# Stated orders at both ends of an attention block, and u-phase products of 512 columns over both token parts

## The chip, the cores and the metric

The kernel runs on one core of one Trainium2 chip. Time is microseconds on the device from launch to end, the median of a few executions. TensorE is called PE (its weight loads PEld), VectorE DVE, ScalarE ACT, GpSimd POOL, and SP is the sync engine, which issues most DMAs.

## The reference, cut to what matters

Two layers follow each other on 256 tokens of width 1024, all in fp32. The first is a feed-forward, a mixer, a second feed-forward and a gate (its code is not touched but for orders). The second is this:

```python
h = modulate(rmsnorm(x, norm1_g), sh1, sc1)
z = h @ w_in                          # u_pool, q, k, v, f_logit, g_a, g_b
y = sigmoid(g_a) * pool_mixer(u_pool) + sigmoid(g_b) * forgetting_attention(q, k, v, log_sigmoid(f_logit + b_f))
x = x + gt1 * (y @ w_out)
h2 = modulate(rmsnorm(x, norm2_g), sh2, sc2)
# peer_ffn: 8 heads, each picks 16 of 16384 experts by product keys
u = expert_u[ec]
a = gelu(einsum('cd,chkd->chk', xc, u), approximate=False) * wc
out = einsum('chk,chkd->cd', a, expert_v[ec])
x = x + gt2 * out
return rmsnorm(x, final_g)
```

## The kernel before

Every fp32 product is made of three: each operand is split into a high part H (rounded by ACT) and a low part L (the rest, by DVE, L289 and L290), and HL, HH and LH add up in PSUM (mm3, L314). Weights come by DMA into raw buffers (SP's queue), wload and wsplit turn them into wh and wl. The tokens are two parts, c = 0 and 1, of 128.

The experts are computed densely. In the u phase (ublock, L1684) block i of 128 multiplies 128 experts' u with all 256 tokens: fm_mm takes 8 steps of three products of 256 columns (L323 to L325), and ACT applies Gelu into row i of the tile G. DVE meanwhile finds the top 16 keys (half, cand, lookup); from about block 45 on, wgroup builds one-hot matrices (onehots, DVE, L1659 to L1662), PE turns them into 4 tokens' routing weights, and DVE multiplies these into the rows of G that are there. td is the number of tokens whose weights are there; for these a block's Gelu goes to a tile and DVE multiplies (L1693). Background work is dealt to the blocks by a credit (UC). Then the v phase multiplies G with expert v.

The order of each engine's instructions is fixed when the program is built, by a planner that simulates the engines; issue_after(x) makes the block's instructions on x's engine follow x in that engine's queue, and behind_split(c) does so after a part's last split. These are orders, not waits on other engines. Engines run their queues in order.

Around attention: ple makes the gate and the normed x; Norm.part, chunk and quads (L450 to L481) square, scale (xs), transpose four tiles into a bank, modulate them (two on ACT, two on DVE) into one tile of 512 columns, and split that into hH and hL. The attention's first product is v (wv, tm_proj with a lag of 5 weights between the parts). At its end out_step multiplies y by the output weights, ev_out adds to x, the next Norm follows, and query_w splits the query weights qw for the first four query tiles. In the query loop QORD gives the order of the first tiles; 0 to 3 are only transposed there. TAIL's last feed-forward products load their weights in ffn.

```python
def behind(f, *a):
    with tc.issue_after(ins_of(lasts["pe"])):
        return f(*a)
```

## Time and profile before

| | us |
|---|---|
| median of 3 runs | 1575.57 |
| lowest, highest | 1574.95, 1575.89 |
| the profiled execution | 1574.45 |
| its span, first to last instruction | 1572.6 |
| PE busy | 1549.9 |
| DVE busy | 1125.7 |
| ACT busy | 806.6 |
| POOL busy | 83.0 |

The span is the profiled execution without what lies around it. Busy shares are averages over stages; PE's matmuls overlap in the records, so that a matmul's price is the distance between starts. A wait stands in brackets behind an instruction, with what ended it.

### The profile page before, as it was taken

To read this page: it belongs to the slowest core of one execution; us is meant where nothing else is said; L and a number is where in the kernel's file an instruction comes from. 1 tells how busy PE (TensorE), PEld (TensorE's weight loads), DVE (VectorE), ACT (ScalarE), POOL (GpSimd) and SP (SyncE) were. 2 spreads that over 40 slices of the span, in tenths; PEclk is the share of its full clock that TensorE was granted. 3 is DMA by queue.
4 is the path that set the end of the run, shared out by engine and by line. 5 is a ranking of instruction groups with operands and counts; after the bars stand their busy time and mean duration, and the time that the engine had idled before them with its cause. 6 is when DMAs were issued, how large, how long until landed. Compare 5 with 4: busy or idle time off the path is not lost.

```text
span 1572.6 us, 27124 instructions
## 1 busy us (share of the span) xinstructions
PE 1549.9 (99%) x10317; PEld 1403.6 (89%) x10317; DVE 1125.7 (72%) x2206; ACT 806.6 (51%) x1533; POOL 83.0 (5%) x147
## 2 busy tenths in 40 slices
PE   9999999999999999999999999999999999999997
PEld 7999999879999879998899999999999877888886
DVE  7767768768866666557799988788986666555654
ACT  6444564554455656655554555544445445554543
POOL 1300011100000112011000000000000000000001
PEclk9999999999999999999999999999999999999999
DMA  8777754438976356442455655555446777666662
GB/s 315 242 259 255 246 170 135 140 104 298 337 227 228 123 189 200 134 135 94 150 162 186 187 175 165 162 158 161 161 158 199 248 227 232 191 190 195 215 189 87
DMA packets 84995, 299.94 MB, mean 191 GB/s; under 512 B 9632, under 2 KB 11264, under 8 KB 84608
## 3 DMA queue, kind: packets, MB, share of 16 engines
q1 hardware_dynamic: 80640, 290.86, 56.6%
q10 hardware_dynamic: 4224, 7.34, 1.4%
q8 instruction: 81, 1.33, 0.3%
q14 instruction: 50, 0.41, 0.1%
HBM read 294.95 MB, written 3.15 MB: 190 GB/s over the span
## 4 chain that ended last, share of the span: by engine, by line
PE 89%; DMA 4%; DVE 3%; ACT 2%; issue 1%; POOL 0%; ACTq 0%; POOLq 0%; DVEq 0%
PE mm L323 15%; PE mm L324 15%; PE mm L325 15%; PE acc L319 12%; PE acc L321 11%; PE acc L320 11%; DMA raw<-in_pv 2%; DMA raw<-in_wmod 2%; DVE wl L290 1%; PE acc L1673 1%; ACT wh L289 1%; PE acc L1674 1%; PE acc L925 1%; PE sc L1290 1%; PE mm L1565 0%
## 5 line engine op out<-in xcount | busy, mean ns | idle before, releaser
L289 ACT ACTIVATE wh<-raw 128x1024 fp32r<-128x1024 f32 (+3 forms) x605 | 528.3, 896 | 539.1 <-PE mm L324 251.9
L290 DVE TENSOR_TENSOR wl<-raw,wh 128x1024 fp32r<-128x1024 f32 (+3 forms) x605 | 611.2, 1027 | 264.7 <-ACT wh L289 260.0
L323 PE MATMUL mm<-hL,wh 128*128 128x256 f32 x1976 | 565.4, 286 | 0.0
L325 PE MATMUL mm<-hH,wl 128*128 128x256 f32 x1976 | 560.2, 284 | 0.0
L324 PE MATMUL mm<-hH,wh 128*128 128x256 f32 x1976 | 560.0, 283 | 0.0
L323 PEld LDWEIGHTS mm<-hL,wh 128*128 128x128 f32 x1976 | 377.6, 191 | 2.7
L324 PEld LDWEIGHTS mm<-hH,wh 128*128 128x128 f32 x1976 | 377.9, 191 | 2.0
L325 PEld LDWEIGHTS mm<-hH,wl 128*128 128x128 f32 x1976 | 377.4, 191 | 0.5
L319 PE MATMUL acc<-wh,aL 128*128 128x512 f32 x648 | 255.9, 395 | 1.6 <-DVE aL L290 1.6
L320 PE MATMUL acc<-wh,aH 128*128 128x512 f32 x648 | 253.0, 390 | 0.0
L321 PE MATMUL acc<-wl,aH 128*128 128x512 f32 x648 | 252.9, 392 | 0.0
L321 PEld LDWEIGHTS acc<-wl,aH 128*128 128x128 f32 x648 | 121.7, 188 | 28.2 <-issue 0.2
L319 PEld LDWEIGHTS acc<-wh,aL 128*128 128x128 f32 x648 | 121.9, 188 | 27.4 <-DVE aL L290 2.8
L320 PEld LDWEIGHTS acc<-wh,aH 128*128 128x128 f32 x648 | 121.8, 188 | 26.2 <-issue 0.5
L319 PE MATMUL acc<-wh,hL 128*128 128x512 f32 x224 | 89.3, 401 | 3.1 <-ACT wh L289 1.7
L320 PE MATMUL acc<-wh,hH 128*128 128x512 f32 x224 | 87.4, 392 | 0.0
L321 PE MATMUL acc<-wl,hH 128*128 128x512 f32 (+1 forms) x224 | 85.8, 391 | 0.0
L624 DVE SCALAR_TENSOR_TENSOR macc<-raw,col,macc 128x1024 f32<-128x1024 f32 x28 | 36.1, 1288 | 29.4 <-DMA raw<-in_wmod 29.3
L290 DVE TENSOR_TENSOR aL<-G,aH 128x256 fp32r<-128x256 f32 x128 | 53.6, 419 | 3.4 <-ACT aH L289 3.4
L319 PEld LDWEIGHTS acc<-wh,hL 128*128 128x128 f32 x224 | 42.5, 190 | 13.0 <-ACT wh L289 3.2
L289 ACT ACTIVATE aH<-G 128x256 fp32r<-128x256 f32 x128 | 51.2, 401 | 4.0 <-PE acc L321 4.0
L587 ACT ACTIVATE sg<-sg 128x256 f32<-128x256 f32 x36 | 14.8, 411 | 71.0 <-DVE sg L586 68.1
(469 smaller groups left out, 1620.9 us busy)
## 6 DMA issues: line engine op xcount, KB each, us to landing
raw<-in_pu SPq DMA_DIRECT2D x128, 512.0 KB, 3.5
raw<-in_pv SPq DMA_DIRECT2D x128, 512.0 KB, 4.3
raw<-in_wmod SPq DMA_DIRECT2D x48, 512.0 KB, 4.8
raw<-in_w1gu SPq DMA_DIRECT2D x36, 512.0 KB, 4.4
raw<-in_w2gu SPq DMA_DIRECT2D x36, 512.0 KB, 4.9
raw<-in_w1d SPq DMA_DIRECT2D x22, 512.0 KB, 4.8
raw<-in_w2d SPq DMA_DIRECT2D x22, 512.0 KB, 4.5
raw<-in_wout SPq DMA_DIRECT2D x16, 512.0 KB, 3.6
```

The costliest lines, as they stand in the source:

```text
L289: lasts["high"] = act.activation(H, src, AF.Copy)
L290: lasts["low"] = dve.tensor_sub(L, src, H.bitcast(F32))
L319: mm_(ps, aL, bH, start=start, stop=False)
L320: mm_(ps, aH, bH, start=False, stop=False)
L321: lasts["pe"] = mm_(ps, aH, bL, start=False, stop=stop)
L323: mm_(ps, aH, bL, start=start, stop=False)
L324: mm_(ps, aH, bH, start=False, stop=False)
L325: mm_(ps, aL, bH, start=False, stop=stop)
L624: dve.scalar_tensor_tensor(macc[j], raw, K("c", k), macc[j], op0=OP.mult, op1=OP.add)
L925: mm_(ps[:, j, c], k[pr][:, j, sl], q[pr][:, j, sl], start=True, stop=True)
L1290: mm_(ps[:, o:o + n], qa[:, hd, c * 128:c * 128 + 128], ka[:, hd, 0:n], start=True, stop=False)
L1673: mm_(ps[:, j], H[:, j], O[:, j], start=True, stop=False)
```

## The change

The u product. ublock uses fm_wide: a weight's high half is multiplied with hH and hL side by side (512 columns, hH in the bank's first half, hL in the second), its low half with hH alone (256). The halves of the bank must then be added. While no routing weights are there (td is 0), ACT copies both halves into two rows of G, POOL adds them, ACT applies Gelu in place. Later ACT copies the second half, DVE adds the first from PSUM, ACT applies Gelu, and POOL, not DVE, multiplies by the routing weights. A block's evacuation comes behind the background work dealt to it. hH and hL become one tile for this, in every norm.

Orders. wv's splits, the scaling of xr, wpool's DMA, the last query weights' splits and ev_out(1, 1) get stated places; a quad's modulated tile becomes two; three of four query weights get their L from POOL; head 15 uses a bank of "sc"; QORD interleaves. The first feed-forward's lag goes from 4 to 2, its and the second's tail weights follow the last split, and x, col and w1t are loaded in another order. Left out of the diff: where hH, hL and yH, yL become halves of one tile.

```diff
@@ -35,8 +35,9 @@
-FLAG = (4, 4)
+FLAG = (2, 4)
 TLW = (3, 3)
+TLA = (2, 2)
@@ -55,7 +56,7 @@
-QORD = [4, 5, 0, 1, 2, 3]
+QORD = [4, 0, 5, 1, 6, 2, 7, 3]
@@ -264,12 +265,12 @@
     xv = A["x"].rearrange("(c p) d -> p c d", p=128)
-    def xload(c, j):
-        nc.sync.dma_start(xr[:, c, j * 512:j * 512 + 512], xv[:, c, j * 512:j * 512 + 512])
...
-    xload(0, 0)
+    def xload(c, a, b):
+        nc.sync.dma_start(xr[:, c, a:b], xv[:, c, a:b])
+    xload(0, 0, 128)
     nc.sync.dma_start(cst[:, 0:128], A["cst"][:, 0:128])
-    nc.scalar.dma_start(col, A["col"])
+    xload(0, 128, 512)
@@ -329,6 +330,19 @@
+    def fm_wide(ps, w, hw, nk=8):
+        for k in range(nk):
+            wH, wL = (w[i][:, k * 128:(k + 1) * 128] for i in range(2))
+            low = lambda: mm_(ps[:, 0], wL, hw[:, 0, k], start=False, stop=False)
+            if k == nk - 1:
+                low()
+            mm_(ps, wH, hw[:, :, k], start=k == 0, stop=k == nk - 1)
+            if k < nk - 1:
+                low()
@@ -437,12 +451,12 @@
         def __init__(self, hp, gain, shift=None):
-            self.hH = hp.tile([128, 8, 256], F32R, tag="hH", name="hH")
-            self.hL = hp.tile([128, 8, 256], F32R, tag="hL", name="hL")
+            self.both = hp.tile([128, 2, 8, 256], F32R, tag="h", name="h")
+            self.hH, self.hL = self.both[:, 0], self.both[:, 1]
             self.gain, self.shift = gain, shift
...
             self.s, self.xs, self.last_xs, self.mp = {}, {}, {}, nxp
-            self.last_hH, self.last_hL = {}, {}
+            self.last_hH, self.last_hL, self.late = {}, {}, {}
@@ -460,25 +474,32 @@
         def quads(self, c):
...
                 self.quad(c, q)
+            for k in list(self.late) if c else ():
+                with self.behind_split(1), tc.high_priority(offset=-300):
+                    self.late.pop(k)()
             return self.last_pe
...
-            sl, qs = slice(c * 128, (c + 1) * 128), slice(4 * q, 4 * q + 4)
+            sl = slice(c * 128, (c + 1) * 128)
             x = self.xs[c]
...
                 self.last_pe = nc.tensor.transpose(bk[:, i], x[:, dt * 128:(dt + 1) * 128], ident)
-            m = self.mp.tile([128, 4, 128], F32, tag="mod", name="mod", bufs=2)
-            for i in range(4):
-                dt = 4 * q + i
-                if i < 2:
-                    act.activation(m[:, i], bk[:, i], AF.Identity, scale=self.gain(dt), bias=self.shift(dt))
-                else:
-                    dve.tensor_scalar(m[:, i], bk[:, i], self.gain(dt), self.shift(dt), op0=OP.mult, op1=OP.add)
-            self.last_hH[c] = act.activation(self.hH[:, qs, sl], m, AF.Copy)
-            self.last_hL[c] = dve.tensor_sub(self.hL[:, qs, sl], m, self.hH[:, qs, sl].bitcast(F32))
+            for u in range(2):
+                m = self.mp.tile([128, 2, 128], F32, tag="mod%d" % u, name="mod", bufs=2)
+                for i in range(2):
+                    dt = 4 * q + 2 * u + i
+                    if u == 0:
+                        act.activation(m[:, i], bk[:, 2 * u + i], AF.Identity, scale=self.gain(dt),
+                                       bias=self.shift(dt))
+                    else:
+                        dve.tensor_scalar(m[:, i], bk[:, 2 * u + i], self.gain(dt), self.shift(dt),
+                                          op0=OP.mult, op1=OP.add)
+                us = slice(4 * q + 2 * u, 4 * q + 2 * u + 2)
+                self.last_hH[c] = act.activation(self.hH[:, us, sl], m, AF.Copy)
+                self.last_hL[c] = dve.tensor_sub(self.hL[:, us, sl], m, self.hH[:, us, sl].bitcast(F32))
@@ -590,6 +611,7 @@
                 aH = p.tile([128, 256], F32R, tag="aH", name="aH", bufs=TAIL[i - 1] + 2)
...
                 split(a, aH, aL)
+                last_a = lasts["high"], lasts["low"]
                 pend.append((f, (aH, aL)))
@@ -598,7 +620,13 @@
             cut["n"] = CUT4[i - 1]
-            W = [wload(wd[f_], 1024, pw if n_ >= len(pend) - TLW[i - 1] else None) for n_, (f_, _) in enumerate(pend)]
+            W = []
+            for n_, (f_, _) in enumerate(pend):
+                with ExitStack() as order_:
+                    if n_ >= TLA[i - 1]:
+                        for a_ in last_a:
+                            order_.enter_context(tc.issue_after(ins_of(a_)))
+                    W.append(wload(wd[f_], 1024, pw if n_ >= len(pend) - TLW[i - 1] else None))
@@ -698,12 +726,13 @@
             q.dma_start(raw1[k][:, i:i + m], A["w1t"][k][:, i:i + m])
     wraw1(0, 2, nc.scalar)
-    wraw1(1, 2, nc.scalar)
-    xload(1, 0)
+    nc.scalar.dma_start(col, A["col"])
+    wraw1(1, 2)
+    xload(1, 0, 512)
     wraw1(2)
-    xload(0, 1)
     wraw1(3)
-    xload(1, 1)
+    xload(0, 512, 1024)
+    xload(1, 512, 1024)
     nc.sync.dma_start(cst[:, 128:], A["cst"][:, 128:])
@@ -1155,6 +1184,8 @@
     def ple(nin, nout):
...
             st, hg = {}, {}
+            squares, sums = nout.squares, nout.sums = {}, {}
+            nout.gates = {}
@@ -1164,7 +1195,7 @@
                 t = p.tile([128, 512], F32, tag="pg", name="pg")
...
                 with nout.behind_split(0) if c else nullcontext():
-                    act.activation(t, ps, AF.Tanh, scale=nin.half[c])
+                    nout.gates[c] = act.activation(t, ps, AF.Tanh, scale=nin.half[c])
                     dve.scalar_tensor_tensor(t, t, 1.0, proj[:, c, sl], op0=OP.add, op1=OP.mult)
@@ -1182,7 +1213,7 @@
                     pool.tensor_scalar(ss[:, 5:6], ss[:, 0:1], EPS, D * EPS * EPS, op0=OP.mult, op1=OP.add)
...
                 else:
-                    act.activation(sq[:, 0:256], g[:, 0:256], AF.Square, accum_out=ss[:, 3:4])
+                    squares[c] = act.activation(sq[:, 0:256], g[:, 0:256], AF.Square, accum_out=ss[:, 3:4])
                     dve.scalar_tensor_tensor(sq[:, 256:], g[:, 256:], 1.0, g[:, 256:], op0=OP.mult, op1=OP.mult,
@@ -1191,14 +1222,19 @@
                 ss = st[c]
-                v = nrm.tile([128, 2], F32, tag="q1", name="q1")
-                dve.tensor_scalar(v[:, 0:1], ss[:, 3:4], ss[:, 4:5], ss[:, 5:6], op0=OP.add, op1=OP.add)
+                v = nrm.tile([128, 1], F32, tag="q1", name="q1")
+                sums[c] = dve.tensor_scalar(v[:, 0:1], ss[:, 3:4], ss[:, 4:5], ss[:, 5:6], op0=OP.add, op1=OP.add)
                 pool.tensor_tensor(v[:, 0:1], v[:, 0:1], mhalf[:, 0:1], op=OP.pow)
                 nout.chunk(c, hg[c], v[:, 0:1])
-                pool.tensor_scalar(v[:, 1:2], ss[:, 0:1], ss[:, 1:2], D * EPS, op0=OP.add, op1=OP.add)
-                pool.tensor_tensor(v[:, 1:2], v[:, 1:2], mhalf[:, 0:1], op=OP.pow)
-                with tc.high_priority(offset=-300), tc.issue_after(ins_of(nout.last_xs[c])):
-                    dve.tensor_scalar(xr[:, c], hg[c], v[:, 1:2], 32.0, op0=OP.mult, op1=OP.mult)
+                u = nrm.tile([128, 1], F32, tag="q2", name="q2")
+                def late():
+                    pool.tensor_scalar(u, ss[:, 0:1], ss[:, 1:2], D * EPS, op0=OP.add, op1=OP.add)
+                    pool.tensor_tensor(u, u, mhalf[:, 0:1], op=OP.pow)
+                    pool.tensor_scalar(u, u, 32.0, None, op0=OP.mult)
+                    act.activation(xr[:, c], hg[c], AF.Copy, scale=u)
+                nout.late[c] = late
@@ -1251,7 +1287,14 @@
         def wv(kt):
-            with tc.issue_after(ins_of(nin.last_xs[0])) if kt < 5 else nin.behind_split(0):
+            with ExitStack() as order_:
+                if kt > 0:
+                    order_.enter_context(tc.issue_after(ins_of(nin.squares[0])))
+                    order_.enter_context(tc.issue_after(ins_of(nin.sums[0] if kt < 2 else nin.last_xs[0])))
+                if kt > 1:
+                    order_.enter_context(nin.behind_split(0))
+                if kt > 2:
+                    order_.enter_context(tc.issue_after(ins_of(nin.gates[1])))
                 return wload(A["wv"][kt])
@@ -1312,7 +1355,7 @@
         def head4(hd, pT, sums):
-            po = bank("mm" if hd >= POM else "pt", (128, 2, 64))
+            po = bank("sc" if hd == 15 else "mm" if hd >= POM else "pt", (128, 2, 64))
@@ -1323,7 +1366,8 @@
             wp = sm.tile([128, 256], F32, tag="wp", name="wp")
-            nc.scalar.dma_start(wp, A["wpool"][:, g * 256:(g + 1) * 256])
+            with nin.behind_split(1) if g < 2 else nullcontext():
+                nc.scalar.dma_start(wp, A["wpool"][:, g * 256:(g + 1) * 256])
@@ -1459,7 +1503,11 @@
                 sl = slice(j * 512, (j + 1) * 512)
-                split(raw[:, sl], H[:, sl], L[:, sl])
+                if i == 0:
+                    split(raw[:, sl], H[:, sl], L[:, sl])
+                else:
+                    act.activation(H[:, sl], raw[:, sl], AF.Copy)
+                    pool.tensor_sub(L[:, sl], raw[:, sl], H[:, sl].bitcast(F32))
             qw.append((H, L))
@@ -1470,12 +1518,13 @@
         query_w(0)
-        with tc.issue_after(ins_of(pT_read)), tc.issue_after(ins_of(ysum)):
+        with tc.issue_after(ins_of(pT_read)):
             query_w(1)
-        with tc.issue_after(ins_of(yhigh)), tc.issue_after(ins_of(ysum)):
+        with tc.issue_after(ins_of(yhigh)):
             query_w(2)
             query_w(3)
-        ev_out(1, 1, acc[1, 1])
+        with tc.issue_after(ins_of(nout.last_hL[0])):
+            ev_out(1, 1, acc[1, 1])
@@ -1682,15 +1731,29 @@
             state["td"] = t0 + 4
         def ublock(i):
-            ps = mm_bank((128, 256))
-            fm_mm(ps, wload(A["pu"][i]), h)
+            ps = mm_bank((128, 2, 256))
+            fm_wide(ps, wload(A["pu"][i]), n6.both)
+            return ps
+        def upart(i, ps):
             td = state["td"]
+            if td == 0:
+                j = 86 + i % 2
+                rows = G[:, i:j + 1:j - i]
+                act.activation(rows, ps, AF.Copy)
+                pool.tensor_add(G[:, i], G[:, i], G[:, j])
+                act.activation(G[:, i], G[:, i], AF.Gelu)
+                assert i < 86
+                state["cur"] = i + 1
+                return
+            u = ps_.tile([128, 256], F32, tag="ge", name="ge")
+            act.activation(u, ps[:, 1], AF.Copy)
+            dve.tensor_add(u, ps[:, 0], u)
             if td < 256:
-                act.activation(G[:, i, td:], ps[:, td:], AF.Gelu)
-            if td > 0:
-                t = ps_.tile([128, 256], F32, tag="ge", name="ge")
-                act.activation(t[:, 0:td], ps[:, 0:td], AF.Gelu)
-                dve.tensor_mul(G[:, i, 0:td], t[:, 0:td], G[:, i, 0:td])
+                act.activation(G[:, i, td:], u[:, td:], AF.Gelu)
+            act.activation(u[:, 0:td], u[:, 0:td], AF.Gelu)
+            pool.tensor_mul(G[:, i, 0:td], u[:, 0:td], G[:, i, 0:td])
             state["cur"] = i + 1
@@ -1711,7 +1774,7 @@
             if i < 16:
...
             else:
-                ublock(0)
+                upart(0, ublock(0))
@@ -1735,8 +1798,9 @@
         for i in range(1, 128):
-            ublock(i)
+            ps = ublock(i)
             run(UC)
+            upart(i, ps)
         while bg:
...
```

## Rows read from the trace of the kernel before

**Rows 1.** The page: busy time and share of each engine; the chain by engine.

```profile
PE 1549.9 (99%) x10317; PEld 1403.6 (89%) x10317; DVE 1125.7 (72%) x2206; ACT 806.6 (51%) x1533; POOL 83.0 (5%) x147
...
PE 89%; DMA 4%; DVE 3%; ACT 2%; issue 1%; POOL 0%; ACTq 0%; POOLq 0%; DVEq 0%
```

**Rows 2.** Busy time by stretch of the u phase: us, engines, PEclk, DMA.

```profile
806.00:898.70 92.70, 92.70 (x775) 92.70 (x774) 88.16 (x368) 47.21 (x70) 0.00 (x0) 1.00 0.58 182
898.70:943.40 44.70, 44.70 (x383) 44.66 (x382) 37.84 (x61) 23.72 (x38) 0.00 (x0) 1.00 0.56 177
946.10:1184.80 238.70, 238.70 (x2230) 236.06 (x2229) 205.02 (x340) 114.62 (x283) 0.00 (x0) 1.00 0.51 160
```

**Rows 3.** Timeline of PE in a u block: start us, us, what.

```profile
899.80 0.28 PE L323 MATMUL mm<-hL,wh 128*128 128x256 f32 x1
...
906.88 0.28 PE L325 MATMUL mm<-hH,wl 128*128 128x256 f32 x1
```

**Rows 4.** Timeline of PE in the v phase.

```profile
1399.77 0.39 PE L320 MATMUL acc<-wh,aH 128*128 128x512 f32 x1
...
1403.89 0.39 PE L320 MATMUL acc<-wh,aH 128*128 128x512 f32 x1
```

**Rows 5.** Start of attention: timelines of PE and DVE, one stretch's busy times.

```profile
553.93 1.95 PE L643 MATMUL fill<-cst,macc 128*128 128x1 f32 x16 [1.84 <-DVE modc L644]
...
568.49 0.50 PE L319 MATMUL acc<-wh,hL 128*128 128x512 f32 x1 [1.28 <-DVE hL L481]
...
547.03 4.90 DVE L290 TENSOR_TENSOR wl<-raw,wh 128x512 fp32r<-128x512 f32 x8
...
553.79 1.36 DVE L479 TENSOR_SCALAR mod<-mm,modc 128x128 f32<-128x128 f32 x4
...
555.50:559.60 4.10, 3.96 (x13) 3.16 (x13) 4.10 (x9) 3.18 (x7) 0.00 (x0) 0.58 0.34 125
```

**Rows 6.** Waits of PE, 725 to 772 us: for what, us, times, longest.

```profile
PE acc L319 <- DVE hL L481: 3.1, 2, 1.7
PE mm L1317 <- DVE gb L1321: 0.7, 1, 0.7
PE mm L1565 <- ACT qT L1557: 0.6, 1, 0.6
PE mm L472 <- DVE xs L458: 0.6, 1, 0.6
PE acc L319 <- DVE yL L1385: 0.6, 1, 0.6
```

**Rows 7.** Waits of PE, 0 to 20 us.

```profile
PE acc L319 <- ACT wh L289: 1.4, 3, 0.7
```

**Rows 8.** Timeline of PE at the mixer's input products, 512 and 384 columns.

```profile
210.03 0.39 PE L319 MATMUL acc<-wh,hL 128*128 128x512 f32 x1
...
210.73 0.33 PE L319 MATMUL acc<-wh,hL 128*128 128x384 f32 x1
...
211.26 1.62 PE L643 MATMUL fill<-cst,macc 128*128 128x1 f32 x14
```

**Rows 9.** Groups of instructions, whole run: count, busy us, mean ns, idle before.

```profile
L586 DVE TENSOR_TENSOR sg<-mm,R 128x256 f32<-128x256 f32 x36 | 15.1, 420 | 5.1 <-PE mm L325 5.1
```

**Rows 10.** Groups of DVE's instructions, 946.1 to 1184.8 us.

```profile
L290 DVE TENSOR_TENSOR wl<-raw,wh 128x1024 fp32r<-128x1024 f32 x72 | 88.1, 1224 | 33.5 <-ACT wh L289 33.5
...
L1693 DVE TENSOR_TENSOR G<-ge,G 128x8 f32<-128x8 f32 (+35 forms) x72 | 20.2, 280 | 0.0
```

**Rows 11.** Timelines of DVE and POOL where a POOL product meets splits; POOL alone.

```profile
607.71 0.69 DVE L290 TENSOR_TENSOR wl<-raw,wh 128x512 fp32r<-128x512 f32 x1
...
608.73 1.83 DVE L290 TENSOR_TENSOR wl<-raw,wh 128x512 fp32r<-128x512 f32 x2
...
608.89 1.11 POOL L1351 TENSOR_TENSOR ga<-ga,y 128x256 f32<-128x256 f32 x1 [1.65 <-DVE y L1350]
...
603.03 0.61 POOL L1337 TENSOR_TENSOR psum__6605<-pu 128x255 f32<-128x255 f32 x1
```

More of the change, by code (lines that the diff above doesn't have):

```diff
@@ L494, in __init__ @@
         def __init__(self, hp, gain):
-            self.hH = hp.tile([128, 8, 256], F32R, tag="hH", name="hH")
-            self.hL = hp.tile([128, 8, 256], F32R, tag="hL", name="hL")
+            self.both = hp.tile([128, 2, 8, 256], F32R, tag="h", name="h")
+            self.hH, self.hL = self.both[:, 0], self.both[:, 1]
             self.gain, self.h = gain, (self.hH, self.hL)
@@ L799, in mixer @@
         vm = m.tile([128, 2, 512], F32, name="vm")
-        yH = hA.tile([128, 8, 256], F32R, tag="hH", name="yH")
-        yL = hA.tile([128, 8, 256], F32R, tag="hL", name="yL")
+        y_ = hA.tile([128, 2, 8, 256], F32R, tag="h", name="yH")
+        yH, yL = y_[:, 0], y_[:, 1]
         latent = {}
@@ L1373, in attention @@
         set_psum(acc=2, mm=2, sc=2, pt=2)
-        yH = hA.tile([128, 8, 256], F32R, tag="hH", name="yH2")
-        yL = hA.tile([128, 8, 256], F32R, tag="hL", name="yL2")
+        y_ = hA.tile([128, 2, 8, 256], F32R, tag="h", name="yH2")
+        yH, yL = y_[:, 0], y_[:, 1]
         def y_tile(dt):
@@ L1764, in peer @@
             if i == 96:
-                hs = [hB.tile([128, 2, 1024], F32R, tag=t, name="w" + t) for t in ("hH", "hL")]
+                hs_ = hB.tile([128, 2, 2, 1024], F32R, tag="h", name="wh_")
+                hs = [hs_[:, 0], hs_[:, 1]]
                 for k in range(2):
```

## Prediction, made before the changed kernel was run

> **What bounds the kernel now.** I read the page's busy shares and chain first. TensorE (PE) is busy 99% of the span and carries 89% of the chain that ended last [rows 1], so a saving counts only where it shortens PE's work or closes a hole in it. Next came stretches by time. The u phase, 128 blocks between 806 and 1208 us, has no PE hole, VectorE (DVE) at 95% in its first 32 blocks and at 86% later, ScalarE (ACT) near half, GpSimd (POOL) at zero [rows 2]. Here a block's price is its matmul count times their spacing, and DVE is the next engine behind. Last came the spacing of matmul starts (a busy PE is no PE at its peak) and PE's waits at the seams. 60 matmuls of 256 columns start in the 7.08 us between two rows, 59 steps of 0.120 us [rows 3]; 18 steps of 512 columns take 4.12 us, 0.229 each [rows 4]. What PE loses by waiting lies at the two ends of the attention block [rows 5, 6] and, less, at the start [rows 7].
>
> **The u product.** A block has 8 steps of 3 products of 256 columns, 3 x 0.120 = 0.360 us a step. fm_wide has one product of 512 (weight high half against both token parts) and one of 256, 0.229 + 0.120 = 0.349 us. So 0.011 us a step, 0.088 a block, **11.3 us** over 128 blocks if PE stays the bound. No run of alternating 512 and 256 columns stands in the trace. The nearest alternates 512 and 384: three of 512 take 0.70 us and three of 384 take 0.53 [rows 8], so each keeps its own spacing and the weight loads stay hidden. That the moving operand is now two pieces a distance apart is not shown; I take it as free, with 0 us of gain as the bound (at 0.240 a wide product, nothing is saved).
>
> The Trainium skill's page "TensorE: Matmul & The Clock Gate" (Back-to-back issue gap) gives a spacing of N/2.4 + 2.5 ns, a much smaller fixed part than the 13 to 16 ns left here after 106.7 and 213.3. By it a step would save 2.5 ns and the phase 2.6 us. The rows decide for the larger figure.
>
> **What it moves to other engines.** Blocks before routing (45 of them): ACT copies 512 columns out of PSUM, POOL adds the two rows of G, ACT applies Gelu. Blocks after (83): ACT copies 256, DVE adds from PSUM, ACT applies Gelu, POOL multiplies instead of DVE. No row prices ACT's 512-column copy; DVE's PSUM pass of 256 columns at 0.42 us [rows 9] puts it between 0.4 and 0.9. ACT is idle (92.70 - 47.21) / 32 = 1.4 us a block [rows 2], so it has room. The copy shares ACT's queue with the next weight split (wh) and the Gelu now waits there for POOL or DVE; queued behind that Gelu are later splits. Three weight buffers are some two blocks of lead, 5.6 us, so I cost this at nothing; if the lead is eaten, each block pays the overrun.
>
> DVE: in the 73 blocks of 946 to 1185 us it is busy 205.0 us [rows 2]. It loses the multiply, 20.2, and gains 73 x 0.42 = 30.7 [rows 9, 10]: 215.5 us, against PE's 238.7 - 73 x 0.088 = 232.3. Slack 16.8 us, 0.23 a block. In the first 32 blocks DVE's own work is unchanged at 88.2 against PE's 92.7 - 2.8 = 89.9: slack 1.7 us, 0.05 a block.
>
> **POOL against DVE** uses up that slack. Alone, a POOL add of 255 columns takes 0.61 us. At 608.89 one met DVE splits of 512 columns: it took 1.11, and the two splits took 1.83 together where one takes 0.69 [rows 11]. So POOL first waited for the running split, and then DVE's next one waited some 0.55 us. Bounds per block: 0 (a following operation that isn't held) to 0.55 (each time), for columns in proportion; the multiply's width grows from 4 to 256, so its mean bound is 0.3. I take 0.07 before routing. POOL's add comes after ACT's copy; about half of DVE's time there is the split (1.22 of 2.75 us a block), and behind it follow searches on one stream. A hit in the other half holds the next split only if that begins within 0.6 us: 0.6 x 0.6 / 2 / 2.79 = 0.065, an estimate that rests on the searches not being held, which no row shows. After routing I take 0.18, half the time a full hold. Then 32 x 0.07 = 2.2 just exceeds the slack of 1.7, and 73 x 0.18 = 13 stays below 16.8. Unevenness between blocks costs some more: I keep **9.5** of 11.3 us.
>
> The Trainium skill's "SBUF — State Buffer" (Who interferes with whom) speaks against this part: a DVE instruction with two SBUF inputs and a GpSimd one that reads SBUF hold a shared port exclusively, the later fully blocked. The rows at 608 agree. Taken at its worst, on every block, it is the slower rival below.
>
> **Start of attention.** PE waits 1.84 us at 553.93, because the modulation of the first token part (DVE, 553.79) sits behind eight split halves of wv that run from 547.03 [rows 5]. After that hole, and sixteen one-column products behind it, the granted clock is 0.58 on the mean of 555.5 to 559.6, so mostly the lower of its two levels, 1.2 and 2.4 GHz [rows 5]: (1 - 0.58) x 4.1 = 1.7 us. A further 1.28 us are lost at 568.49 for the second part's hL. The change puts wv's splits from kt 2 on behind the first part's split, moves the scaling of xr from DVE to ACT and out of the way, and halves the modulation tiles. The moved splits are then late next: PE needs a wv every 1.37 us (six products of 0.229), DVE makes one in 1.2 [rows 10], beside the second part's norm. The splits hold their raw buffers longer, so SP's loads of later wv wait for them; wp's DMA goes behind the second split and is needed far later. Of 4.8 us I take **3.5**; bounds +1 (starved of wv) and -4.8.
>
> **End of attention.** PE waits 3.1 us for hL, 0.7 for head 15's bank, 0.6 for yL, 0.6 for xs [rows 6]. Halving the quads lets the first half of hH and hL start after two modulations, not four (0.7 us of the 1.36 [rows 5]) and with passes of half the width (0.3 us each on ACT and DVE, an estimate from 0.69 for 512 columns [rows 11]): about 1.2 us for each of the two parts. Head 15 gets its own bank, and DVE loses six splits of qw. These go to POOL, at twice 0.61 about 1.2 us each, 7 us, in front of the norm's small POOL steps; xr's adds have two SBUF inputs and may be held. Of 5.0 us I take **3.0**; bounds +1.5 and -4.5.
>
> **Small ones.** At the start PE waits 1.4 us for wh [rows 7]. A first x piece of a quarter, w1t before col on ACT's queue, w1t 1 on SP's and a lag of 2 may close it, while col, now behind, feeds the first scaling: I take 0.5 (bounds +1, -1.4). Interleaving the short queries with long ones touches the 0.6 us wait for qT [rows 6]: 0.5 (bounds 0, -0.8). The tail loads of the feed-forward only get an order behind the last split; PE's work queued there hides them: nothing, or up to 1 us if a split comes late.
>
> **Sum** against the profiled execution, 1574.45 us (span 1572.6 and 1.85 around it): -9.5 - 3.5 - 3.0 - 0.5 - 0.5 = -17.0, 1557.5. The median stands 1.1 above it: **1559 us**.
>
> **The rivals.**
> Slower: DVE becomes the u phase's bound because POOL holds it in every block. For: the phase's first 32 blocks have 0.05 us of slack, and the rows at 608. Against: the searches have one stream, and the multiply is short at first. Price: 32 blocks at 88.2 + 17.6 = 105.8 against 92.7, +13.1; the next 13, 37.8 + 7.2 = 45 against 44.7, +0.3; the 73, 215.5 + 22 = 237.5 against 238.7, -1.2; the last ten, some +1 for bunching. It decides once the hold passes 0.05 us a block before routing. With the seams' -7.5 it gives +6, and with the seams at half, +10: 1582 to 1586, 1583 as its time. Chance 0.14.
> The u phase gives nothing (DVE and PE in balance, or the wide product at 0.240): -7.5, 1568. For: slack after routing is 0.23 us a block on average, less where lookups fall. Chance 0.15, a third of it with weak seams, near no change.
> The seams give nothing, a new wait (wv late, POOL's queue) taking the place of each old one: -9.5, 1566. For: both seams fill DVE almost wholly. Chance 0.15.
> Spacing with a 2.5 ns fixed part at either width: the u phase saves 2.6, in all -10.1, 1565. Against it stand both spacings. Chance 0.05. (The rule of the TensorE page.)
> The forecast has 0.48, with its own range of 1553 to 1565; 0.03 is left for no change by mishaps.
>
> **How the numbers follow.** With every bound met the sum is -11.3 - 4.8 - 4.5 - 1.4 - 0.8 = -22.8, 1551.6 and at the median 1552.8; 1552 is the low end. The high end leaves out most of the slower rival and takes in a u phase with half its hold and seams at nothing: 1579. A measurement of this kernel tells 0.2%, about 3 us, from no change. Faster: 0.48 + 0.15 + 0.05 + 0.10 = 0.78, less a little, 0.77. Same: 0.05 + 0.03 + 0.01 = 0.09. Slower: 0.14.
>
> **What would show it.** Spacing in the u phase of 0.229 and 0.120 in turn, and blocks of 2.79 us before routing; PE holes there with releaser DVE wl would mean the lock. DVE splits longer than 1.22 us beside POOL rows count its price. At 552 us PE should go on without a hole and at a full clock; a wait for wl there would be the new one. At 749 and 757 the waits for hL should halve. The prediction is wrong if blocks take 2.88 us or more.

## The result, and the profile after

The changed kernel takes 1584.1 us in the median of 6 runs (1580.73 to 1586.59), the kernel before 1575.26 us on the same chip: **slower by 0.56%, ratio 1.0056 [1.0044, 1.0068]**. Forecast were 1559 us and a gain. Its profiled execution took 1582.17 us (span 1580.3), 7.7 us more than the one of before.

The page of the changed kernel, busy time and share by engine, answers to [rows 1]:

```profile
PE 1550.5 (98%) x9293; PEld 1348.1 (85%) x9293; DVE 1152.3 (73%) x2207; ACT 869.0 (55%) x1673; POOL 217.4 (14%) x283
...
PE 90%; DMA 3%; DVE 3%; ACT 2%; issue 1%; POOL 0%; ACTq 0%; POOLq 0%; DVEq 0%
```

PE has 1024 products fewer and is busy as long as before: a product's busy time overlaps the next one's, so it tells nothing of the gain. PE still bounds. Two stretches of the u phase (busy us by engine, PEclk, DMA; [rows 2]) and a timeline of PE inside it ([rows 3, 4]):

```profile
820.00:898.00 78.00, 78.00 (x446) 67.94 (x445) 74.86 (x322) 55.44 (x88) 20.56 (x27) 1.00 0.55 180
952.00:1190.00 238.00, 238.00 (x1685) 204.99 (x1684) 229.47 (x352) 148.37 (x361) 68.71 (x73) 1.00 0.50 163
```
```profile
879.69 0.40 PE L343 MATMUL mm<-h,wh 128*128 128x512 f32 x1
...
885.33 0.40 PE L343 MATMUL mm<-h,wh 128*128 128x512 f32 x1
```

PE has no hole there and the clock is full, though DVE is at 96%. The two starts are 16 steps apart: 5.64 / 16 = 0.3525 us a step, where 0.360 stood before and 0.349 was costed.

PE's waits in the other stretches: 0 to 20 us ([rows 7]), 180 to 200 us (before: none), 550 to 580 us ([rows 5]), 735 to 800 us ([rows 6]); what waited, for what, us in total, times, longest:

```profile
PE mm L527 <- DMA xr<-in_x: 1.7, 1, 1.7
PE acc L320 <- ACT wh L290: 1.6, 1, 1.6
```
```profile
PE acc L320 <- ACT wh L290: 2.4, 1, 2.4
```
```profile
PE mm L489 <- DVE xs L472: 3.6, 1, 3.6
```
```profile
PE mm L1614 <- ACT qT L1606: 3.0, 4, 1.1
PE acc L320 <- DVE yH L1429: 2.4, 1, 2.4
PE acc L320 <- DVE h L502: 1.8, 2, 0.9
```

The old holes are gone or halved (552 us, head 15's bank, hL at 749 and 757), and each seam has a new one. To add them up with the slower clock behind them, take **PE's loss** in a stretch: the sum of the distances between neighbouring starts, less 0.229 us behind a product of 512 fp32 columns, 0.120 behind one of 256, and the median of its form behind any other. A loss near 0 means that PE ran at its best spacing. Worked out from the PE rows of each trace, in us (before_again is a second profile of the kernel before; the other names are the experiments'):

```
                        0-20  180-200  540-580  700-800  800-1220
before                   2.9    -0.1      5.6      8.5       3.3
before_again             2.6    -0.1      5.6      8.5       3.3
the changed kernel       5.6     4.4      6.3     13.2       8.4
u_alone                  4.3     5.1      6.7      8.6       8.7
u_again                  3.4     7.4      6.7      8.5       8.7
orders_alone             3.9     0.3      6.2     13.3       3.3
four_off                 2.9     2.9      5.3      8.2       8.7
four_off_again           2.6     6.9      6.3      8.2       8.6
start_off                2.9     3.1      5.3     13.2       8.4
qord_off                 5.7     1.9      5.3     10.2       8.4
qw_on_dve                5.0     0.6      4.9     11.3       8.4
tail_order_off           4.4     6.3      4.4     11.7       8.4
```

With 11.3 us costed off the u phase, the changed kernel's losses there and at the seams stand 5.1 + 2.7 + 4.5 + 0.7 + 4.7 = 17.7 us above those of before: +6.4 of the 7.7 us.

### The profile page after: what moved, and what is told of

The parts are those of the page before. It is cut to its first block, busy times and chain, and to the rows that moved or that the text cites. A ratio compares the mean times of both kernels' runs of the same rounds, so it can differ in the third digit from the quotient of the medians.

```text
span 1580.3 us, 25425 instructions
## 1 busy us (share of the span) xinstructions
PE 1550.5 (98%) x9293; PEld 1348.1 (85%) x9293; DVE 1152.3 (73%) x2207; ACT 869.0 (55%) x1673; POOL 217.4 (14%) x283
## 4 chain that ended last, share of the span: by engine, by line
PE 90%; DMA 3%; DVE 3%; ACT 2%; issue 1%; POOL 0%; ACTq 0%; POOLq 0%; DVEq 0%
PE mm L343 15%; PE acc L320 13%; PE acc L322 12%; PE acc L321 12%; PE mm L340 8%; PE mm L324 7%; PE mm L325 7%; PE mm L326 7%; DMA raw<-in_wmod 2%; DVE wl L291 2%; PE acc L1722 1%; ACT wh L290 1%; PE acc L1723 1%; PE acc L954 1%; PE sc L1333 1%
## 5 line engine op out<-in xcount | busy, mean ns | idle before, releaser
L343 PE MATMUL mm<-h,wh 128*128 128x512 f32 x1024 | 359.9, 399 | 0.0
L324 PE MATMUL mm<-h,wh 128*128 128x256 f32 (+1 forms) x952 | 271.4, 285 | 0.0
L326 PE MATMUL mm<-h,wl 128*128 128x256 f32 (+1 forms) x952 | 270.1, 284 | 0.0
L340 PE MATMUL mm<-h,wl 128*128 128x256 f32 x1024 | 268.9, 283 | 1.0 <-DVE wl L291 1.0
L325 PE MATMUL mm<-h,wh 128*128 128x256 f32 (+1 forms) x952 | 269.4, 283 | 0.0
L343 PEld LDWEIGHTS mm<-h,wh 128*128 128x128 f32 x1024 | 186.1, 188 | 33.2
L340 PEld LDWEIGHTS mm<-h,wl 128*128 128x128 f32 x1024 | 193.2, 189 | 12.8 <-DVE wl L291 3.1
L324 PEld LDWEIGHTS mm<-h,wh 128*128 128x128 f32 (+1 forms) x952 | 181.3, 190 | 2.8
L325 PEld LDWEIGHTS mm<-h,wh 128*128 128x128 f32 (+1 forms) x952 | 181.3, 190 | 2.3
L326 PEld LDWEIGHTS mm<-h,wl 128*128 128x128 f32 (+1 forms) x952 | 181.2, 190 | 0.4
L320 PE MATMUL acc<-wh,h 128*128 128x512 f32 (+1 forms) x224 | 89.7, 404 | 1.9 <-ACT wh L290 1.9
L321 PE MATMUL acc<-wh,h 128*128 128x512 f32 (+1 forms) x224 | 88.4, 397 | 0.0
L322 PE MATMUL acc<-wl,h 128*128 128x512 f32 (+1 forms) x224 | 85.6, 394 | 0.0
```

The lines of the kernel that those rows point to most:

```text
L320: mm_(ps, aL, bH, start=start, stop=False)
L321: mm_(ps, aH, bH, start=False, stop=False)
L322: lasts["pe"] = mm_(ps, aH, bL, start=False, stop=stop)
L324: mm_(ps, aH, bL, start=start, stop=False)
L325: mm_(ps, aH, bH, start=False, stop=False)
L326: mm_(ps, aL, bH, start=False, stop=stop)
```

## The experiments

Ratios are to the kernel before, timed on the same chip, with 95% intervals. 0.001 is 1.6 us.

### The u products alone, the orders alone

u_alone is the kernel before with the three new pieces of the u phase:

```diff
-            ps = mm_bank((128, 256))
-            fm_mm(ps, wload(A["pu"][i]), h)
+            ps = mm_bank((128, 2, 256))
+            fm_wide(ps, wload(A["pu"][i]), n6.both)
+            return ps
...
-            ublock(i)
+            ps = ublock(i)
             run(UC)
+            upart(i, ps)
```

> The kernel before with the new u products alone (fm_wide, upart, hH and hL as halves of one tile); every order as before. Theory (the u phase gained, the orders lost): in the two traces the stretch from the last qw product to the v phase took 445.0 us before and 441.8 after, with 2.9 us of new waits for qT inside it, so the u phase gave about 6.1 us and this kernel takes 1575.3 - 6 = 1569 us (1565 to 1571). Rival (POOL holding DVE eats the gain, the orders cost little): 1575 us or more, with PE waits for wl in the blocks.

orders_alone is the changed kernel with these lines and ublock's evacuation as before.

> The changed kernel with the u products as before; all of the new orders stay. Theory: the orders cost 13.8 us up to the end of the query stage, so 1575.3 + 13.8 = 1589 us (1586 to 1592), 5 to 6 us slower than the changed kernel. Rival (the u phase is what lost): 1575 to 1580, faster than the changed kernel.

Measured: u_alone **1573.33 us, 0.9993 [0.9982, 1.0003]**; orders_alone **1583.07 us, 1.0053 [1.0038, 1.0068]**. That the orders are what loses is the theory's reading, but its size was not: 8.3 us, where 13.8 were said and 1586 us was its least. The u products bring 1 us, between the two readings, with an interval that takes in no change. In their own stage they do gain; timelines of PE, last qw product and first product of the v phase, of before and of u_alone:

```profile
762.81 0.39 PE L321 MATMUL acc<-qw,hH 128*128 128x512 f32 x1
...
1207.81 0.39 PE L319 MATMUL acc<-wh,aL 128*128 128x512 f32 x1
```
```profile
770.56 0.40 PE L321 MATMUL acc<-qw,h 128*128 128x512 f32 x1
...
1209.67 0.40 PE L319 MATMUL acc<-wh,aL 128*128 128x512 f32 x1
```

445.0 us before, 439.1 here: 5.9 us less. But the last qw product starts 7.8 us later, and of that 5.2 us are lost at 180 to 200 us (and 1.4 at 0 to 20, 1.1 at 540 to 580). That is in the first feed-forward, where the two programs are the same instruction for instruction, waits included.

### Loads that land late in the first feed-forward

> The kernel before with the u products alone, profiled a second time. Its instructions up to 235 us stand in the order of the kernel before on PE, ACT, DVE and SP, and yet its first profile had a hole of 2.4 us at 192 us (loads landing late in the feed-forward's tail) that the kernel before does not show. Theory (a load stream near its limit, whose lateness differs from one execution to the next): the hole's length differs by over 1 us between the two profiles of this same kernel. Rival (something of the u products makes the loads late every time): a hole of 2.4 us again, pT issued at 181.7 us again. In both the stretch from the last qw product to the v phase is 439 us, as in the first.

> The kernel before, profiled a second time. Its first profile shows no PE hole between 180 and 200 us and pT issued at 176.6 us; the two profiles of the kernel with the u products alone show 5.1 and 7.4 us lost there and pT at 181.7 and 182.6, with the same instructions in the same order up to then. Theory (the lateness of this load stream differs from one execution to the next): here a loss of 1 us or more at 180 to 200 us, or pT over 1 us off 176.6. Rival (it belongs to the kernels with the new u products): under 0.3 us lost, pT at 176 to 177.

u_again lost 7.4 us there, before_again nothing, with pT issued at 182.6 and 174.2 us. Each run bears out something of both readings. The lateness does differ between executions: u_alone and u_again, one program, lost 5.1 and 7.4 us, and the issue of pT in the kernel before moved by 2.4 us. But whether PE loses anything there goes with the program. Here the issues of DMAs (KB each, median us to landing) between 40 and 170 us, of before and of u_again:

```profile
raw<-in_w1gu SPq DMA_DIRECT2D x28, 512.0 KB, 4.3
raw<-in_w1d SPq DMA_DIRECT2D x18, 512.0 KB, 4.7
```
```profile
raw<-in_w1gu SPq DMA_DIRECT2D x29, 512.0 KB, 4.6
raw<-in_w1d SPq DMA_DIRECT2D x16, 512.0 KB, 5.1
```

As I read it, weights that take 0.3 us longer delay the buffers they sit in, and so SP's next loads; by the tail the stream is 5 us behind, and ACT's and DVE's splits of late weights stand ahead of the last gate. Is it the new products that do this?

```diff
-            fm_mm(ps, wload(A["pu"][i]), h)
+            w = wload(A["pu"][i])
+            for k in range(8):
+                mm_(ps, w[0][:, k * 128:(k + 1) * 128], h[0][:, k], start=k == 0, stop=False)
+                mm_(ps, w[1][:, k * 128:(k + 1) * 128], h[0][:, k], start=False, stop=k == 7)
```

> The kernel before with the third product of each u step (weight high half by hL) left out, so that its output is off by that part; no other change, and every engine's instructions up to the u phase at 800 us are the same as before. Theory (the loads of the first feed-forward land late in any program that is built otherwise later on): 2 us or more lost at 180 to 200 us, weight loads of the feed-forward (40 to 170 us) landing in 4.6 us or more on the mean, against 4.50 and 4.46 in the two profiles of the kernel before and 4.74 and 4.89 with the new u products alone. Rival (it belongs to the new u products themselves, or was chance): nothing lost there, 4.4 to 4.5 us.

Its SP and PE timelines (pT's load; PE's start with its wait), beside SP's of before:

```profile
180.03 0.33 SPq L294 DMA_DIRECT2D raw<-in_pT  x1
...
193.44 0.80 PE L319 MATMUL acc<-wh,aL 128*128 128x512 f32 x1 [3.17 <-DVE aL L290]
```
```profile
176.57 0.33 SPq L294 DMA_DIRECT2D raw<-in_pT  x1
```

6.6 us lost, loads at 4.72 us on the mean (4.50 and 4.46 in the two profiles of the kernel before), in one profile. So it isn't the new products: a program that is the same for its first 800 us and other behind them has its loads landing later in the first 200. The length of PE's program was the first candidate.

```diff
                 done(c, j * 512, j * 512 + 512, acc[c][j], g2)
+        ps = mm_bank((128, 8))
+        with tc.issue_after(ins_of(lasts["pe"])):
+            for q in range(1024):
+                mm_(ps[:, q % 8:q % 8 + 1], C("ones", 0, 128), C("ones", 0, 1), start=True, stop=True)
```

> The kernel before with the new u products alone, and 1024 products of one column put behind the last product of the program, so that PE's program is as long again as in the kernel before; all that stands ahead of them is the same (the time grows by the length of these products and is not compared). Theory (the length of PE's program decides whether the first feed-forward's loads land late): under 0.3 us lost at 180 to 200 us, loads landing in 4.5 us on the mean. Rival (another difference between the programs, or chance): 2 us or more lost there, 4.6 us or more.

4.3 us lost, 4.64 us: the length doesn't decide. Nor are there more loads of instructions: between 40 and 170 us each of these traces has 7 or 8 packets on the larger of the two queues for them. The profiles were taken on several chips, but the timings of u_alone and of the kernel before, on one chip, differ by only 1 us where the u stage gained 5.9. **Why the loads land late in these programs stays open.** Nor is late landing the whole story: the changed kernel's loads, which start in another order, land in 4.52 us on the mean, those of tail_order_off in 4.56, and yet 4.4 and 6.3 us are lost there.

What it costs was tried by moving four loads away, M0 from 20 to 16, on the best version (below) and on the kernel before.

> The version with four orders undone, with M0 at 16: four of the 20 wmod loads that run through the first feed-forward (2 MB, about 8 us of its load stream) move to the second. Theory (that stream is near its limit, and its tail lands late): the hole at 190 us, 2.9 us with the clock behind it, goes, 1572.5 - 3 = 1569.5 us or less. Rival (the loads are late whatever is queued ahead of them, or the second feed-forward now has the hole): 1572.5 us or more.

> The kernel before with M0 at 16 and nothing else. Theory (the kernel before has no such hole to lose): within 1 us of the kernel before, 1575 us. Rival (fewer loads help by themselves): 1572 us or less, which would then also explain a gain of the run with four orders undone.

The first: 0.9994 [0.9984, 1.0004]. The hole at 190 us is gone (loss 0.2), but 2 us are lost anew at 47 us and 2 at 560, so no gain: the rival's time, by new holes. The second: 1.0019 [1.0010, 1.0027], slower by 3 us, outside both expectations. It loses 7.2 us at 540 to 580, 1.6 more than the kernel before, and 1.3 more at 20 to 100: the moved loads cost more where they go.

### Four orders undone, together and one by one

four_off undoes TLA, the start (FLAG and the loads), QORD and POOL's L of the query weights:

```diff
-FLAG = (2, 4)
+FLAG = (4, 4)
-TLA = (2, 2)
+TLA = (9, 9)
-QORD = [4, 0, 5, 1, 6, 2, 7, 3]
+QORD = [4, 5, 0, 1, 2, 3]
-    xload(0, 0, 128)
+    xload(0, 0, 512)
     nc.sync.dma_start(cst[:, 0:128], A["cst"][:, 0:128])
-    xload(0, 128, 512)
+    nc.scalar.dma_start(col, A["col"])
...
-    nc.scalar.dma_start(col, A["col"])
-    wraw1(1, 2)
+    wraw1(1, 2, nc.scalar)
...
-                if i == 0:
-                    split(raw[:, sl], H[:, sl], L[:, sl])
-                else:
-                    act.activation(H[:, sl], raw[:, sl], AF.Copy)
-                    pool.tensor_sub(L[:, sl], raw[:, sl], H[:, sl].bitcast(F32))
+                split(raw[:, sl], H[:, sl], L[:, sl])
```

> The changed kernel with four orders undone: the tail weights (TLA), the start (FLAG, x, col and w1t), QORD, and L of the query weights from POOL. The u products and the orders at both ends of attention stay. Theory: 4.4 + 2.7 + 2.9 + 2.0 = 12.0 us come back, 1584.1 - 12.0 = 1572 us (1569 to 1575). Rival (these seams only trade places with what follows, or the spread of the changed kernel is its u phase's): 1580 to 1584.

**1572.55 us, 0.9981 [0.9971, 0.9991]**: 11.8 us below the changed kernel, where the theory had 12.0. In part that is luck: by PE's loss 2.7 us came back at the start and 5.0 at 700 to 800 us, as it said, but only 1.5 of the 4.4 at 180 to 200, and 1.0 at 540 to 580 that it did not have. Each alone, from the changed kernel:

> The changed kernel with TLA at (9, 9): the tail weights of the feed-forwards follow no stated order, as before. Theory (the splits held behind the last split keep the raw buffers, so pT and wpp land late and block ACT and DVE ahead of the last gate): the 2.4 us hole at 192 us and the lower clock behind it go, 4.4 us in all, 1584.1 - 4.4 = 1579.7 us, and SP issues pT some 4 us earlier. Rival (the hole comes from the lag of 2 in FLAG or from the loads being late in any order): the hole stays, 1584.

> The changed kernel with the start as before: FLAG at (4, 4), x in pieces of 512, col ahead of w1t, w1t 1 on ACT's queue. Theory (each seam's loss in the trace is lost in the end too): PE's wait for the second x piece at 4.7 us and a part of the wait for wh go, 2.7 us, 1584.1 - 2.7 = 1581.4 us. Rival (one of the four undone orders carries most of the 11.5 us that they are worth together): either 1584, or under 1578 where the start is that one.

> The changed kernel with QORD as before. Theory: the four waits for qT between 776 and 793 us (3.6 us of PE waits in all, against one of 0.6 before) go, 1584.1 - 2.9 = 1581.2 us. Rival: 1584 where the waits only move to a later step, or under 1578 where this is the order that carries most of the 11.5 us.

> The changed kernel with L of all query weights made by DVE as before, none by POOL. Theory (POOL's subtractions hold DVE's yL split and its add to xr for 1.1 us each, 1.77 and 1.79 where 0.69 is usual): both take 0.69 again, the 2.4 us wait for yH at 747 us shrinks to 1.3 or less, and the clock behind it falls less: 1584.1 - 2.0 = 1582 us. Rival (the six splits more on DVE stand ahead of the norm, as before): 1584 or more. Third reading: under 1578 where this order carries most of the 11.5 us.

```
                 ratio    interval             us against 1.0056   in its own stretch
tail_order_off   1.0049   [1.0033, 1.0065]     -1.1                +1.9
start_off        1.0002   [0.9989, 1.0016]     -8.5                -2.7
qord_off         1.0028   [1.0016, 1.0039]     -4.4                -3.0
qw_on_dve        1.0036   [1.0024, 1.0047]     -3.2                -1.9
```

The tail order is not what makes the hole at 192 us: without it 6.3 us are lost there, and my first reading of the trace was wrong. (Profiles of one program differ there by 2 to 4 us, so the +1.9 is no price.) The four add up to 17.2 us where the four together gave 11.8, so at least one of them is not worth what it shows alone. QORD and the query weights cost about what their stretch shows; the waits of 765 to 800 us in qord_off, and of 735 to 770 in qw_on_dve:

```profile
PE mm L1614 <- ACT qT L1606: 0.6, 1, 0.6
```
```profile
PE acc L320 <- DVE yH L1429: 1.3, 1, 1.3
```

One wait for qT instead of four of 3.0, and yH 1.3 instead of 2.4. Where POOL's subtractions hold DVE is seen in the changed kernel's timelines of DVE and POOL ([rows 11]):

```profile
744.17 3.57 DVE L291 TENSOR_TENSOR wl<-raw,wh 128x512 fp32r<-128x512 f32 x4
747.66 0.41 DVE L1429 TENSOR_TENSOR yH<-mm,yH 128x256 fp32r<-128x256 f32 x1
...
750.17 1.79 DVE L1435 TENSOR_TENSOR xr<-gt,xr 128x512 f32<-128x512 f32 x1
```
```profile
745.82 5.59 POOL L1510 TENSOR_TENSOR qw<-raw,qw 128x512 fp32r<-128x512 f32 x4 [4.11 <-ACT qw L1509]
```

Four splits take 3.57 us, where four take 2.49 at 567.05 (a row shown below), and the add to xr takes 1.79 where 0.69 is usual: one of the four splits, and the add, are each held by 1.1 us while POOL's row runs. yH, which has one input in PSUM, takes its usual 0.41 beside it. The Trainium skill's "SBUF — State Buffer" (Who interferes with whom) says that a DVE instruction with two SBUF inputs contends with a GpSimd one that reads SBUF, by an exclusive lock; the trace agrees, with 1.1 us for each of these two.

The start is the odd one: 8.5 us in time, 2.7 in its stretch. Two kernels took it apart. lag_off undoes FLAG alone, x_in_one_piece the split of the first x piece alone:

```diff
-    xload(0, 0, 128)
+    xload(0, 0, 512)
...
-    xload(0, 128, 512)
```

> The changed kernel with FLAG alone at (4, 4), the lag of the first feed-forward as before; x, col and w1t still in the new order. With both undone the kernel took 0.54 percent less than the changed one, about 8 us. Theory (a lag of 2 leaves the first down product less lead over its loads, and the lead is then short for the whole of the feed-forward): 1584.1 - 6 = 1578 us or less. Rival (the load order: the second x piece lands late, and PE starts its first products late and at the lower clock): over 1581 us, and the wait at 4.7 us stays in either case.

> The changed kernel with its first load of x in one piece of 512 columns again instead of 128 and 384; col, w1t and the other pieces stay in the new order. Theory (the second piece, behind cst on SP's queue, lands at 6.6 us and starts PE's lateness): the wait at 4.7 us goes, 1584.1 - 3 = 1581 us or less. Rival (w1t 1 on SP's queue behind x, and the first w1t alone on ACT's, make wh late): the wait moves to wh at 7 to 9 us, 1584 us.

lag_off: 1.0054 [1.0041, 1.0067], so the lag is nothing. x_in_one_piece: 1.0024 [1.0014, 1.0033], 5 us less, the time that the theory had; but its wait moves as the rival said, from x to wh, and its loss at 0 to 20 us stays (5.8). Waits of 0 to 20 us in x_in_one_piece and in start_off:

```profile
PE acc L319 <- ACT wh L289: 4.0, 1, 4.0
```
```profile
PE acc L320 <- ACT wh L290: 1.0, 3, 0.7
```

The profiled execution of x_in_one_piece, 1584.84 us, is the slowest of its 11, so its trace does not show where the 5 us come from. Of the start's 8.5 us the lag is then nothing and the small x piece some 5; about 3 are left for the places of the other first loads (col, w1t, the later x pieces), which no run varied alone. Only 2.7 us are seen at PE in the first 20 us, and the profiled executions of start_off and of the changed kernel are only 4.5 us apart: the way of the rest is not shown.

### The start of attention, and the wide product

wv_order_off is four_off with wv's splits in the order of before.

```diff
-            with ExitStack() as order_:
...
-                return wload(A["wv"][kt])
+            with tc.issue_after(ins_of(nin.last_xs[0])) if kt < 5 else nin.behind_split(0):
+                return wload(A["wv"][kt])
```

> The version with four orders undone, with wv's splits too in the order of the kernel before (the first five behind the first part's xs, the rest behind its split). Theory (the order only trades the hole at 552 us for one of the same size at 568, where the second part's norm stands among the wv splits): a hole of 1.8 us at 554 us again, the wait for xs at 568 gone or below 1.3, and the same time, 1572.5 us within 1.5. Rival (the forecast's term): 3.5 us slower than the version with four orders undone, 1576 us.

0.9992 [0.9982, 1.0002], 1573.86 us: the theory's time, with a hole of 1.2 us where it had 1.8. PE's waits of 540 to 580 us in it, and in four_off:

```profile
PE fill L671 <- DVE modc L672: 1.2, 1, 1.2
PE acc L320 <- DVE h L502: 0.9, 1, 0.9
PE mm L489 <- DVE xs L472: 0.6, 1, 0.6
```
```profile
PE mm L489 <- DVE xs L472: 3.7, 1, 3.7
```

Losses 4.9 and 5.3 us: three small holes against one large. Where the large one comes from, in the changed kernel's DVE timeline, and the clock behind it, 0.51 and so almost all at the lower of its two levels, 1.2 and 2.4 GHz:

```profile
567.05 2.49 DVE L291 TENSOR_TENSOR wl<-raw,wh 128x512 fp32r<-128x512 f32 x4
569.46 0.41 DVE L1217 SCALAR_TENSOR_TENSOR sq<-hg 128x256 bf16<-128x256 f32 x1
...
572.23 0.88 DVE L472 TENSOR_SCALAR xs<-hg,q 128x512 f32<-128x512 f32 x2 [1.62 <-POOL q L1227]
```
```profile
572.70:578.00 5.30, 5.23 (x17) 4.42 (x18) 3.21 (x10) 4.03 (x10) 0.00 (x0) 0.51 0.05 19
```

The second part's square stands behind wv's splits, POOL's power behind that, xs at its end; PE is through with the wv products queued ahead of it by 568.7 us.

wide_in_one_piece is four_off with hH and hL of a step side by side:

```diff
-            self.both = hp.tile([128, 2, 8, 256], F32R, tag="h", name="h")
-            self.hH, self.hL = self.both[:, 0], self.both[:, 1]
+            self.both = hp.tile([128, 8, 2, 256], F32R, tag="h", name="h")
+            self.hH, self.hL = self.both[:, :, 0], self.both[:, :, 1]
```

> The version with four orders undone, with hH and hL of a step side by side, so that a wide product's 512 columns are one piece instead of two that lie 2048 columns apart; the instructions and their order are the same. In the two traces with the new u products a wide product and the low one behind it take 0.2352 + 0.1176 = 0.3528 us where 0.229 + 0.120 = 0.349 was costed. Theory (the two pieces cost it): 0.349 a step, 1024 x 0.0038 = 3.9 us less, 0.9981 - 0.0025 = 0.9956 of the kernel before, 1568.6 us. Rival (the change of width between two products costs it): 0.3528 again, 1572.5 us.

Its 16 steps between two rows take 886.19 - 880.55 = 5.64 us, 0.3525 a step again:

```profile
880.55 0.40 PE L343 MATMUL mm<-h,wh 128*128 128x512 f32 x1
...
886.19 0.40 PE L343 MATMUL mm<-h,wh 128*128 128x512 f32 x1
```

The two pieces cost nothing; the rival, the change of width, is left, but was not varied by itself. The time, 0.9999 [0.9987, 1.0010], is 2 us above four_off's with the same instructions in the same order. So four_off was timed again:

> The version with four orders undone, measured a second time. Theory (it is faster than the kernel before by 0.1 to 0.3 percent, the u products' 6 us less what the loads and the ends of attention take back): 0.998 again, 1572 us beside 1575. Rival (measurements of this kernel scatter by 0.2 percent from one chip or session to the next): 0.9995 or more.

0.9991 [0.9982, 1.0000], between the two readings. Both measurements put it below the kernel before, by 3 and 1.4 us; it is the best of the versions, by hardly more than can be told.

## Why the prediction was wrong, step by step

**The u product's spacing** was mis-sized. Costed: 0.229 + 0.120 = 0.349 us a step, from products of one width [rows 3, 4]. Measured: 0.3525, so 7.7 us over 1024 steps, not 11.3. [rows 8] had it: three of 512 in 0.70 are 0.233 each, not 0.229, in a row of alternating widths; I read it as "keeps its own spacing". The forecast's sign of being wrong, blocks of 2.88 us, did not come: a block takes 8 x 0.3525 = 2.82. The Trainium skill's "TensorE: Matmul & The Clock Gate" (Back-to-back issue gap) gives N/2.4 + 2.5 ns for products taken singly, which would make the pair 0.325 us, an estimate; the trace does not agree, with 0.3525.

**POOL against DVE** was sized about right and cost PE little. Groups of instructions at 950 to 1180 us ([rows 9, 10]):

```profile
L291 DVE TENSOR_TENSOR wl<-raw,wh 128x1024 fp32r<-128x1024 f32 x72 | 89.0, 1236 | 2.6 <-ACT wh L290 2.4
L1752 DVE TENSOR_TENSOR ge<-mm,ge 128x256 f32<-128x256 f32 x71 | 29.4, 413 | 4.9 <-ACT ge L1751 4.9
...
L1756 POOL TENSOR_TENSOR G<-ge,G 128x4 f32<-128x4 f32 (+35 forms) x71 | 67.0, 948 | 166.9 <-ACT G L1730 145.7 <-ACT ge L1755 15.9 <-DVE G L1672 3.0
```

The add is 0.413 us (0.42 costed); the splits grow from 1224 ns to 1236, and to 1260 before routing, one row of one-hot products from 0.69 us to 0.89 (L1659, now L1708). In all DVE is busy 229.5 us in the 238 us shown above, where 215.5 + 13 were costed. PE waited once for wl, 1.0 us. The slower rival's mechanism did not occur, and that its time, 1583 us, did is luck. In its stage the u phase gained 5.9 us (u_alone) of the 9.5 forecast; of the 1.8 between that and the 7.7 of the spacing, a single wait for wl at 944 us, as routing begins, cost 1.5.

**The step that failed altogether** is one I did not write: that a gain in the u phase leaves the first 800 us as they are. The programs with it lose 0.6 to 7.4 us at 190 us (0.2 where four loads were moved away), those with the u phase of before at most 0.3, and u_alone ends 1 us below before. The rival "the u phase gives nothing" had that result, for another reason.

**The seams.** The rival "the seams give nothing, a new wait taking the place of each old one" had their mechanism, a chance of 0.15; its price, nothing, was too small: all orders together cost 8.3 us.

**Attention's start**, -3.5 taken: the hole at 552 us and its clock went, as said; the wait that came is not the one I named as next (wv late) but the second part's norm, queued behind wv's splits. Worth nothing (wv_order_off). I listed these splits "beside the second part's norm" and priced them by PE's pace, not by what stands behind them.

**Attention's end**, -3.0 taken: halved quads and the bank worked (the losses ahead of h's first products, 1.9 and 1.5 us before, became 1.0 and 1.1, and the bank's wait went), but splits that stand in DVE's queue now make yH late (1.3 us, even in four_off), so that the seam as a whole gave 0.3 us there (a loss of 8.2 for 8.5). POOL's subtractions cost 1.9 in the stretch, 3.2 in time. I had named this lock for xr's add and put it inside a bound; it was near certain, since POOL's row of 5.6 us spans what DVE does there.

**QORD**, -0.5 taken, bounds 0 and -0.8: +3.0 in its stretch. The bounds excluded a loss without a reason. With the short queries (0 to 3) back to back PE waited once for a transposed copy (0.6 us); alternated with long ones, four times (3.0 us). That back to back they hide each other's copies is my reading, not shown.

**The start**, -0.5 taken, bound +1: about +8 in time, 2.7 at PE. A smaller first piece didn't help here, where the second one, behind cst on the same queue, landed at 6.6 us. **The tail order** at nothing was right within its interval.

So of -17.0, the u term came out at -1 in all, and the orders at +8.3 where -7.5 was taken.

## What to carry to other kernels

Price each moved instruction by what is queued behind it on its engine, up to the next thing PE waits for; here a hole that closed because work was moved opened again where the work went, at each seam. A bound that excludes a loss needs a reason, for an order most of all. Two programs alike for 800 us differed by 5 us within the first 200, so judge an edit by its own stretch as well as by the time, and time the same code twice before believing 0.2%.

## What the runs showed of the hardware

Where products of 512 and 256 columns alternate, the narrow one starts 0.235 us behind the wide one, where 0.229 is the spacing of wide ones alone, and the next wide one 0.1175 us behind the narrow one, where narrow ones alone have 0.120 (means of 174 and 173 distances at 830 to 900 us in u_alone). Programs whose instructions are equal up to 800 us, and that differ behind, had weights landing in 4.46 and 4.50 us (the kernel before, two profiles) against 4.64 to 4.89 (four profiles of three others), means between 40 and 170 us; the length of PE's program is not the cause, and none was found.

A hole does not always cost the clock. Behind waits of 0.5 and 2.2 us in u_alone, at 190 and 192 us, the granted clock was 0.66 on the mean of the next 5 us, in part the lower of its two levels; behind one of 2.4 us at the same place in four_off it stayed at the upper:

```profile
194.30:199.30 5.00, 4.96 (x15) 3.95 (x16) 2.70 (x5) 1.20 (x3) 0.74 (x1) 0.66 0.78 285
```
```profile
192.90:198.00 5.10, 5.10 (x22) 4.13 (x23) 3.79 (x7) 2.25 (x5) 0.71 (x1) 1.00 0.69 226
```
